# More held weights and an urgent last token block in a hybrid encoder layer: 40 slots instead of 24, the last block's norm ahead of other work, first products in k tiles

## The chip, the cores and the metric

The kernel runs on one core of a Trainium2 chip. The metric is device time in microseconds of one execution, as the median of several. The engines have one instruction queue each, which they work off in order: TensorE (PE; PEld is its weight load), VectorE (DVE), ScalarE (ACT), GpSimd (POOL) and SyncE (SP, here used to issue DMAs).

## The reference, cut to what matters

One encoder layer on 512 tokens of width 1024: two token mixers (windowed attention and a dilated mixture), merged by learned gates, then a layer norm, then a SwiGLU channel mixer with 2816 hidden columns, and a second layer norm.

```python
gates = jax.nn.sigmoid(h @ w_gate[l] + b_gate[l])
g_a, g_b = jnp.split(gates, N_BRANCH, axis=-1)
mixed = g_a * (o_a @ w_br_a[l]) + g_b * (o_b @ w_br_b[l])
y = mixed @ w_out[l]
h = layer_norm(DN_ALPHA * h + y, ln1_g[l], ln1_b[l])
f = (jax.nn.silu(h @ w_ff_gate[l]) * (h @ w_ff_up[l])) @ w_ff_down[l]
h = layer_norm(DN_ALPHA * h + f, ln2_g[l], ln2_b[l])
```

All of it is float32. The kernel writes each float32 operand as a high part and a low part and forms a product from three matmuls (high by high, high by low, low by high).

## The kernel before, in words

**A planner sets the order.** The kernel doesn't issue its instructions as it is written. It records operations (class Program, L95) with the engines they may run on, a cost for each engine, a priority (lower goes first), and what they read and write. The function run (L186) then plays a list schedule: at each moment it gives every free engine the ready operation of the lowest priority that fits the buffer limits, and emits it. So an engine's order comes out of the modelled costs, the priorities and the limits; on the chip each engine keeps that order and waits for whatever isn't there yet. There are limits on several classes of slots; "whl" is the number of slots that hold high and low parts of weights.

**The stretch that the change touches** begins after the mixers. First come the branch products with the gates (L930 to L944). Then comes w_out with the first layer norm (tok_major, L963): the tokens are four blocks t = 0 to 3 of 128, and each block has two column halves j = 0, 1 of 512. The last five of w_out's eight k tiles are taken block by block, so that a block's sum ends while the next ones are still computed. A block's norm is a chain on DVE with one step on ACT: residual (L998) and statistics (L1001) for either half, then the aggregate (L1004), the square root on ACT (L1006), the subtraction of the mean times the gain (L1012) for either half, the reciprocal (L1015), and the last step times reciprocal plus bias (L1023) for either half.

**turn_h1** (L1034) then turns each half into channel-major form: four 128 by 128 transposes on PE into one PSUM bank (L1042); the negated values as a high part (minus, L1050 on ACT or L1052 on DVE) and a low part (L1062, DVE); and two float32 copies by ACT into the tiles h1f (emitted at L322). The negated parts feed products on plain token halves; the h1f tiles are made into the sums and differences T1 to T4 (token_forms, L1095).

**The channel mixer** takes the hidden columns in 22 tiles of 128 (class Quad). A quad replaces the eight block products of a 2 by 2 splitting (columns and token halves) by seven, A11, A12, S1, S2, S3, S4 and A22, each 12 matmuls of 256 columns on weights or sums of weights; their token operands are B11, B21, T1, T2, T3, B22 and T4. A product is recorded in product (L1176), its matmuls stand at L1186 to L1188. Sums of weights, low parts of weights and the combinations of products all run at L1082 on DVE (tt); high parts run on ACT at L322. Some weight sums are accumulated by a DMA from POOL (L1140). The first three quads (N_HALF = 3) go in step: all their A11 and A12, then all S1, all S2 and so on. From quad 3 on they follow one by one, with pieces of the down projection (class Chunk) in between. T1 needs token block 3, while A11 and A12 need only blocks 0 and 1.

At the start of the branches free_all (L897) sets the limit of "whl" to 4 x 5 + 4 = 24. At the first silu of the channel mixer (L1211) it is set to 20. The PE order at the block that matters here was: A11 and A12 of quad 0, of quad 1, A11 of quad 2, the transposes of token block 3, A12 of quad 2, and then S1 of quad 0.

Of the kernel before, what the change touches and what calls it, by code (L numbers as in the profile page):

```python
# [16 lines left out]
S = 512  # L17
# [4 lines left out]
NR = 4  # L22
# [36 lines left out]
FIRST = {("k", 0): (-1000, -998.2, -997.2), ("q", 0): (-998.8, -998.1, -997.1), ("v", 0): (-998.7, -998, -997),  # L59
         ("k", 1): (-996.9,), ("q", 1): (-996.7,), ("v", 1): (-996.6,),  # L60
         "x": (-999.9, -998.5, -997.5, -996.95, -996.8, -996.5, -996.4, -996.3)}
N_WS, N_WHL, N_ATT = 6, 12, 16


N_CHUNK, N_PAIR, N_WF, N_WS2, N_WHL2 = 3, 3, 9, 9, 20
# [23 lines left out]


class Op:
    __slots__ = ("alts", "fn", "prio", "left", "ready", "succ", "bufs", "new", "done", "eng", "strict", "moves")


class Program:  # L95


    def __init__(self, limits):
        self.limits = limits
        self.used = {k: 0 for k in limits}  # L100
        self.ops = []
        self.writer, self.readers = {}, {}
        self.T = 0.0
        self.spare = SPARE
        self.strict = False

    @staticmethod
    def buf_of(tok):
# [1 line left out]

    def op(self, alts, fn, reads=(), writes=(), prio=0.0, after=(), abs_prio=None, moves=0.0):
        o = Op()
        o.alts, o.fn = alts, fn
        o.prio = (self.T + prio if abs_prio is None else abs_prio, len(self.ops))
        o.ready, o.done, o.eng = 0.0, None, None
        deps = set(a for a in after if a is not None)
        for t in reads:
            deps.update(self.writer.get(t, ()))
        for t in writes:
            deps.update(self.writer.get(t, ()))  # L120
            deps.update(self.readers.get(t, ()))
        deps.discard(o)
        for t in reads:
            self.readers.setdefault(t, []).append(o)
        for t in writes:
            self.writer[t] = [o]
            self.readers[t] = []
        o.bufs, o.new = [], []
        o.strict, o.moves = self.strict, moves
        for t in list(reads) + list(writes):  # L130
            b = self.buf_of(t)
            if b not in o.bufs:
                o.bufs.append(b)
# [32 lines left out]
    def run(self):  # L166
# [28 lines left out]
        while n_left:  # L195
            if not times:
                self.stuck(pending)
            now = heapq.heappop(times)
            while times and times[0] <= now:
                heapq.heappop(times)  # L200
            while frees and frees[0][0] <= now:
                _, _, b = heapq.heappop(frees)
                for key in b.keys:
                    if key in self.limits:
                        self.used[key] -= 1
            progress = True
            while progress:
                progress = False
                for e in engines:
                    if free[e] > now:  # L210
                        continue
                    best = None
                    for o in pending[e]:
                        if o.ready <= now and (best is None or o.prio < best.prio) and self.fits(o):
                            if e == DVE and len(o.alts) > 1 and free[ACT] < now + BIAS:
                                continue
                            best = o
                    if best is None:
                        continue
                    o = best  # L220
                    cost = dict(o.alts)[e]
                    for a, _ in o.alts:
                        pending[a].remove(o)
                    for b in o.bufs:
                        if b.tile is None:
                            b.tile = b.make()
                            for key in b.keys:
                                if key in self.limits:
                                    self.used[key] += 1
                    o.fn(e)  # L230
                    o.eng = e
                    if e == SP:
                        end = now + 0.06
                        dma[0] = max(dma[0], now) + 0.45
                        dma[1] = max(dma[1], dma[0] + 0.65) + cost
                        o.done = dma[1] + 0.9
                    elif o.moves:
                        end = now + cost
                        dma[1] = max(dma[1], end) + o.moves
                        o.done = dma[1] + 2.0  # L240
                    else:
                        end = now + cost
                        o.done = end
                    free[e] = end
                    heapq.heappush(times, end)
                    for b in o.bufs:
                        b.users -= 1
                        b.end = max(b.end, o.done)
                        if b.users == 0:
                            heapq.heappush(frees, (b.end + HOP, id(b), b))  # L250
                            heapq.heappush(times, b.end + HOP)
                    for q in o.succ:
                        same = len(q.alts) == 1 and q.alts[0][0] == e and e != SP and not o.moves
                        hop = SAME * (e in (ACT, DVE)) if same else HOP_PE if q.alts[0][0] == PE else HOP
# [26 lines left out]
def hybrid_layer(ctx: ExitStack, tc: tile.TileContext, wpack, xT, xtok, sink, bgate,  # L281
# [51 lines left out]
    def cp_alts(n, ps=False):  # L333
        return [(ACT, act(n, ps)), (DVE, dve(n, not ps))]
# [560 lines left out]
        step(w)  # L895

    def free_all(e):  # L897
        pr.limits.update(gen=N_SLOT - N_WS2 - N_WHL, ws=N_WS2, whl=max(N_WHL, 4 * N_LAST1 + 4))
        pr.spare = SPARE2

    op([(POOL, 0.0)], free_all, after=lasts)
# [61 lines left out]
    def tok_major(nk, last, us_of, u0, g, b, finish, fine, alpha=ALPHA):  # L963
# [22 lines left out]
                    kmm(k, t, j, 0, S, us, wu)  # L986
        res = [(k, us_of(k), unit(u0 + k)) for k in range(nk - last, nk)]
        for t in range(NR):
            st = stats()
            pieces = [(0, 0, S), (1, 0, S)]  # L990
            toks = []
# [28 lines left out]
            for (j, c0, c1), tok in zip(pieces, toks):  # L1020
                z = xt[t, j]
                op([(DVE, dve(c1 - c0, extra=0.06))], lambda e, z=z, st=st, j=j, c0=c0, c1=c1:
                   nc.vector.scalar_tensor_tensor(  # L1023
                       z.t[:, c0:c1], z.t[:, c0:c1], st.t[:, 35:36], b[j].t[:, c0:c1], op0=ALU.mult,
                       op1=ALU.add), reads=[tok, (st, "r"), b[j]], writes=[tok], prio=NOW)
                finish(t, j, c0, c1, tok)

    def copy_by_act(dst, src, n, ps, reads, writes, prio=EV):
        op([(ACT, act(n, ps))], lambda e: copy(ACT, dst(), src()), reads=reads, writes=writes, prio=prio)
# [5 lines left out]
    def turn_h1(t, j, c0, c1, tok):  # L1035
# [16 lines left out]
                nc.vector.tensor_scalar(h1h4[j].t[:, :, c], src(), -1.0, None, op0=ALU.mult)  # L1052

        alone = (j, t // 2) != (0, 1)
        if alone:
            op(cp_alts(S, True), minus, reads=[pb], writes=[(h1h4[j], t)], prio=NOW)
        for kk in range(2):
            x = h1f[j, t // 2][kk]
            copy_by_act(lambda x=x: x.t.rearrange("p (k c) -> p k c", k=2)[:, :, (t % 2) * P:(t % 2) * P + P],
                        lambda kk=kk: src()[:, 2 * kk:2 * kk + 2], 2 * P, True, [pb], [(x, t % 2)], NOW)  # L1060
        if alone:
            op([(DVE, dve(S, extra=0.1))], lambda e: nc.vector.scalar_tensor_tensor(  # L1062
                h1l4[j].t[:, :, c], src(), -1.0, f32(h1h4[j].t[:, :, c]), op0=ALU.mult, op1=ALU.subtract),
               reads=[pb, (h1h4[j], t)], writes=[(h1l4[j], t)], prio=NOW)

    lg, lb = ln_vectors(ln1g, ln1b, begin)
    tok_major(KD, N_LAST1, lambda k: sm[k], U_OUT, lg, lb, turn_h1, False)
# [31 lines left out]
    def token_forms():  # L1099
# [13 lines left out]
            tt(lambda: dst.t, lambda: x.t, lambda: y.t, ALU.subtract, al(x) + al(y), al(dst), S, prio)  # L1113

        p1, p2, p3, p4 = LOOK_T
        for x11, x12 in zip(b11, b12):
            diff(x11, x12, x11, p1)
        TP["T1"] = hl2(b11, p1)
        for x11, x12, x22 in zip(b11, b12, b22):
            diff(x12, x12, x22, p2)  # L1120
            diff(x22, x22, x11, p2)
# [22 lines left out]
    class Quad:  # L1144
# [33 lines left out]
        def product(self, s, b, ps, tok, c, first):  # L1178
            h, l = self.A[s]
            bh, bl, toks = tokens_of(b)  # L1180

            def go(e):
                o = ps.t[:, c]
                for k in range(4):
                    wh, wl = h.t[:, k * P:(k + 1) * P], l.t[:, k * P:(k + 1) * P]
                    mm(o, wh, bh[k](), start=(first and k == 0), stop=False, skip_group_check=True)  # L1186
                    mm(o, wh, bl[k](), start=False, stop=False, skip_group_check=True)  # L1187
                    mm(o, wl, bh[k](), start=False, stop=(k == 3), skip_group_check=True)  # L1188

            op([(PE, 12 * pe(HP))], go, reads=[h, l, *toks], writes=[(ps, tok)])  # L1190
            pr.T += 12 * pe(HP)

        def step(self, n):
            y, xz, t, v = self.y, self.xz, self.t, self.v
# [277 lines left out]
```

## Time and profile before

| | |
|---|---|
| median of 3 runs | 794.45 us (794.45 to 794.64) |
| the profiled execution | 793.29 us, span 791.5 us |
| granted TensorE clock | 0.997 |
| PE busy | 777.4 us, 98% |
| DVE busy | 665.9 us, 84% |
| ACT busy | 463.8 us, 59% |

A timeline row gives the start and the duration in us, the engine, the line and operation, output and inputs, partitions by elements, how many instructions the row holds, and in brackets the idle time ahead of it and what ended it. Matmuls overlap, so that the distance between two starts, not a duration, says what one of them costs PE. Groups of waits give the waiting line, the line waited for, the total in us, how many times, and the longest.

### The profile page before, as it was taken

To read this page: it belongs to the slowest core of one execution; us is meant where nothing else is said; L and a number is where in the kernel's file an instruction comes from. 1 tells how busy PE (TensorE), PEld (TensorE's weight loads), DVE (VectorE), ACT (ScalarE), POOL (GpSimd) and SP (SyncE) were. 2 spreads that over 40 slices of the span, in tenths; PEclk is the share of its full clock that TensorE was granted. 3 is DMA by queue.
4 is the path that set the end of the run, shared out by engine and by line. 5 is a ranking of instruction groups with operands and counts; after the bars stand their busy time and mean duration, and the time that the engine had idled before them with its cause. 6 is when DMAs were issued, how large, how long until landed. Compare 5 with 4: busy or idle time off the path is not lost.

```text
span 791.5 us, 13449 instructions
## 1 busy us (share of the span) xinstructions
PE 777.4 (98%) x4634; PEld 688.3 (87%) x4634; DVE 665.9 (84%) x1410; ACT 463.8 (59%) x1016; POOL 116.4 (15%) x284
## 2 busy tenths in 40 slices
PE   9999999999999999999999999999999999999995
PEld 6788888888998888888888889999999999999984
DVE  5998999899756999675585999988888889788888
ACT  5656675765855675795241487755655655555720
POOL 0000100000034000700011011034112330123000
PEclk9999999999999999999999999999999999999998
DMA  8524122421132122448343377779876977699202
GB/s 270 196 94 140 53 74 68 147 67 67 54 95 67 53 69 93 160 123 289 124 118 66 95 206 202 192 178 211 214 197 148 227 200 210 165 225 207 60 1 106
DMA packets 61125, 109.42 MB, mean 138 GB/s; under 512 B 7041, under 2 KB 8705, under 8 KB 61057
## 3 DMA queue, kind: packets, MB, share of 16 engines
q1 hardware_dynamic: 49392, 87.53, 33.8%
q0 software_dynamic: 11520, 20.98, 16.2%
q8 instruction: 36, 0.59, 0.3%
q14 instruction: 33, 0.26, 0.1%
q10 hardware_dynamic: 144, 0.07, 0.0%
HBM read 104.35 MB, written 4.19 MB: 137 GB/s over the span
## 4 chain that ended last, share of the span: by engine, by line
PE 84%; DVE 10%; DMA 2%; ACT 1%; issue 1%; SPq 1%; DVEq 0%; ACTq 0%
PE ps L443 11%; PE ps L445 11%; PE ps L444 11%; PE ps L1186 7%; PE ps L1188 7%; PE ps L1187 7%; DVE sl L1082 5%; PE ps L1313 4%; PE ps L1314 4%; PE ps L1315 4%; PE ps L621 3%; PE ps L528 2%; PE ps L527 2%; DMA sl<-wpack 2%; PE ps L976 1%; PE ps L974 1%
## 5 line engine op out<-in xcount | busy, mean ns | idle before, releaser
L322 ACT ACTIVATE sl<-sl 128x512 fp32r<-128x512 f32 (+3 forms) x421 | 234.2, 587 | 95.5 <-DVE sl L469 34.8
L1082 DVE TENSOR_TENSOR sl<-sl,sl 128x512 fp32r<-128x512 f32 (+3 forms) x308 | 171.6, 603 | 8.5 <-ACT sl L322 7.6
L322 ACT ACTIVATE sl<-ps 128x256 f32<-128x256 f32 (+5 forms) x189 | 83.3, 456 | 92.5 <-PE ps L1188 58.3
L443 PE MATMUL ps<-x,sl 128*128 128x512 f32 x336 | 133.6, 398 | 0.1
L444 PE MATMUL ps<-x,sl 128*128 128x512 f32 x336 | 131.6, 392 | 0.4 <-DVE x L419 0.2
L445 PE MATMUL ps<-x,sl 128*128 128x512 f32 x336 | 131.4, 391 | 0.0
L1186 PE MATMUL ps<-sl,sl 128*128 128x256 f32 x352 | 99.7, 283 | 0.9 <-ACT sl L322 0.9
L1187 PE MATMUL ps<-sl,sl 128*128 128x256 f32 x352 | 99.8, 284 | 0.8 <-DVE sl L1082 0.8
L1188 PE MATMUL ps<-sl,sl 128*128 128x256 f32 x352 | 99.6, 283 | 0.0
L343 DVE TENSOR_TENSOR sl<-sl,sl 128x512 fp32r<-128x512 f32 x130 | 87.1, 685 | 8.0 <-ACT sl L322 5.8
L1140 POOL DMA_DIRECT2D sl<-wpack x44 | 41.0, 1023 | 255.2 <-DVE sl L1082 107.4
L1186 PE MATMUL ps<-x,sl 128*128 128x256 f32 x264 | 75.0, 284 | 1.1 <-ACT sl L322 1.0
L445 PEld LDWEIGHTS ps<-x,sl 128*128 128x128 f32 x336 | 63.1, 188 | 13.8 <-DVE sl L371 0.2
L1187 PE MATMUL ps<-x,sl 128*128 128x256 f32 x264 | 74.7, 283 | 0.0
L1188 PE MATMUL ps<-x,sl 128*128 128x256 f32 x264 | 74.7, 283 | 0.0
L444 PEld LDWEIGHTS ps<-x,sl 128*128 128x128 f32 x336 | 63.3, 188 | 12.0 <-DVE x L419 1.3
L443 PEld LDWEIGHTS ps<-x,sl 128*128 128x128 f32 x336 | 63.2, 188 | 11.8 <-ACT x L322 1.0
L1186 PEld LDWEIGHTS ps<-sl,sl 128*128 128x128 f32 x352 | 67.5, 192 | 2.0 <-ACT sl L322 1.1
L1187 PEld LDWEIGHTS ps<-sl,sl 128*128 128x128 f32 x352 | 67.5, 192 | 1.8 <-DVE sl L1082 1.2
L1188 PEld LDWEIGHTS ps<-sl,sl 128*128 128x128 f32 x352 | 67.5, 192 | 0.0
L1082 DVE TENSOR_TENSOR sl<-sl,ps 128x512 f32<-128x512 f32 (+1 forms) x78 | 47.2, 610 | 23.1 <-PE ps L1188 14.4
L1186 PEld LDWEIGHTS ps<-x,sl 128*128 128x128 f32 x264 | 50.6, 192 | 2.0 <-ACT sl L322 1.5
(128 smaller groups left out, 1669.4 us busy)
## 6 DMA issues: line engine op xcount, KB each, us to landing
sl<-wpack SPq DMA_DIRECT2D x243, 256.0 KB, 4.0
sl<-wpack POOLq DMA_DIRECT2D x44, 256.0 KB, 5.5
wf<-wpack SPq DMA_DIRECT2D x36, 256.0 KB, 4.4
wf<-wpack POOLq DMA_DIRECT2D x36, 256.0 KB, 7.5
sl<-xT SPq DMA_DIRECT2D x8, 256.0 KB, 5.4
gz<-sl SPq DMA_DIRECT2D x8, 256.0 KB, 2.2
sl<-gz SPq DMA_DIRECT2D x8, 256.0 KB, 4.2
sl<-xtok SPq DMA_DIRECT2D x8, 256.0 KB, 5.4
```

What stands on the lines that cost most here:

```text
L322: nc.scalar.activation(dst, src, AF.Copy)
L343: op([(DVE, dve(S))], lambda e: nc.vector.tensor_tensor(l.t, src.t, f32(h.t), op=ALU.subtract), reads=[src, h], writes=[l], prio=prio, abs ...
L443: mm(o, a, x0, start=(k == 0), stop=False)
L444: mm(o, a, x1, start=False, stop=False)
L445: mm(o, b, x0, start=False, stop=(k == nk - 1))
L1082: op([(DVE, dve(w))], lambda e: nc.vector.tensor_tensor(dst(), x(), y(), op=o), reads=reads, writes=writes, prio=prio)
L1140: return op([(POOL, 1.0)], lambda e: nc.gpsimd.dma_start(dst.t, wpack[u, :, j * S:(j + 1) * S], accum_op=ALU.add), reads=[dst], writes=[ds ...
L1186: mm(o, wh, bh[k](), start=(first and k == 0), stop=False, skip_group_check=True)
L1187: mm(o, wh, bl[k](), start=False, stop=False, skip_group_check=True)
L1188: mm(o, wl, bh[k](), start=False, stop=(k == 3), skip_group_check=True)
L1313: mm(ps.t, x0, w[0].t, start=(first and m == 0), stop=False, skip_group_check=True)
L1314: mm(ps.t, x0, w[1].t, start=False, stop=False, skip_group_check=True)
```

## The change

There are four parts. The limit on held weight slots is 40 instead of 24 from the branches on. Operations of the last token block in tok_major, its transposes and h1f copies, and T1 carry a flag `urgent`: the planner doesn't start an operation without the flag on an engine if a flagged one of lower priority number becomes ready there before the first would end. In turn_h1 the two h1f copies are recorded ahead of the negation, and the negated parts of the last block get a later priority. The products A11 and A12 of the first three quads are recorded as four operations of three matmuls, one for each k tile, where they were one operation of twelve.

```diff
-N_WS, N_WHL, N_ATT = 6, 12, 16
+N_WS, N_WHL, N_ATT, N_WHL1 = 6, 12, 16, 40
...
         o = Op()
+        o.urgent = self.urgent
...
                     cost = dict(o.alts)[e]
+                    if not o.urgent and any(q.urgent and now < q.ready < now + cost and q.prio < o.prio
+                                            for q in pending[e]):
+                        continue
...
-        pr.limits.update(gen=N_SLOT - N_WS2 - N_WHL, ws=N_WS2, whl=max(N_WHL, 4 * N_LAST1 + 4))
+        pr.limits.update(gen=N_SLOT - N_WS2 - N_WHL, ws=N_WS2, whl=N_WHL1)
...
         for t in range(NR):
+            pr.urgent = t == NR - 1
             st = stats()
...
                 finish(t, j, c0, c1, tok)
+        pr.urgent = False
...
         alone = (j, t // 2) != (0, 1)
-        if alone:
-            op(cp_alts(S, True), minus, reads=[pb], writes=[(h1h4[j], t)], prio=NOW)
         for kk in range(2):
             x = h1f[j, t // 2][kk]
             copy_by_act(lambda x=x: x.t.rearrange("p (k c) -> p k c", k=2)[:, :, (t % 2) * P:(t % 2) * P + P],
                         lambda kk=kk: src()[:, 2 * kk:2 * kk + 2], 2 * P, True, [pb], [(x, t % 2)], NOW)
+        pr.urgent = False
         if alone:
+            later = LOOK_T[1] - 1 if t == NR - 1 else NOW
+            op(cp_alts(S, True), minus, reads=[pb], writes=[(h1h4[j], t)], prio=later)
             op([(DVE, dve(S, extra=0.1))], lambda e: nc.vector.scalar_tensor_tensor(
                 h1l4[j].t[:, :, c], src(), -1.0, f32(h1h4[j].t[:, :, c]), op0=ALU.mult, op1=ALU.subtract),
-               reads=[pb, (h1h4[j], t)], writes=[(h1l4[j], t)], prio=NOW)
+               reads=[pb, (h1h4[j], t)], writes=[(h1l4[j], t)], prio=later)
+        pr.urgent = t == NR - 1
...
         p1, p2, p3, p4 = LOOK_T
+        pr.urgent = True
         for x11, x12 in zip(b11, b12):
             diff(x11, x12, x11, p1)
         TP["T1"] = hl2(b11, p1)
+        pr.urgent = False
...
-            def go(e):
+            def go(e, ks=range(4)):
...
-            op([(PE, 12 * pe(HP))], go, reads=[h, l, *toks], writes=[(ps, tok)])
-            pr.T += 12 * pe(HP)
+            n = 1 if s in ("A11", "A12") and self.f < N_HALF else 4
+            for k in range(0, 4, n):
+                op([(PE, 3 * n * pe(HP))], lambda e, k=k: go(e, range(k, k + n)), reads=[h, l, *toks], writes=[(ps, tok)])
+                pr.T += 3 * n * pe(HP)
```

What this does to the order shows at three places. The lines of the changed kernel lie 5 to 13 higher: L998 is L1004, L1001 is L1007, L1012 is L1018, L1023 is L1029, L1042 is L1049, L1062 is L1070, L1082 is L1091, L1186 is L1197, L1211 is L1224, L322 is L327.

DVE, from the second half's statistics of token block 3 to the end of its norm, before. L1082 rows are low parts of weights, st is the block's statistics, and the two sl tiles at L1012 and L1023 are the block's halves:

```order
L1001 BN_STATS st_5114<-sl_4448 128x6
L1082 TENSOR_TENSOR sl_5084<-sl_4825,sl_5083 128x512
L1004 BN_AGGR st_5114<-st_5114 128x2
L1082 TENSOR_TENSOR sl_5092<-sl_4851,sl_5091 128x512
L1012 SCALAR_TENSOR_TENSOR sl_4446<-sl_4446,st_5114,sl_4450 128x512
L1012 SCALAR_TENSOR_TENSOR sl_4448<-sl_4448,st_5114,sl_4452 128x512
L1015 RECIPROCAL st_5114<-st_5114 128x1
L1082 TENSOR_TENSOR sl_5099<-sl_4856,sl_5098 128x512
L1023 SCALAR_TENSOR_TENSOR sl_4446<-sl_4446,st_5114,sl_4454 128x512
L1023 SCALAR_TENSOR_TENSOR sl_4448<-sl_4448,st_5114,sl_4456 128x512
```

And now, with the low part of block 2 (L1070) within the chain, and behind it the one weight split and the two differences of T1:

```order
L1007 BN_STATS st_5168<-sl_4655 128x6
L1010 BN_AGGR st_5168<-st_5168 128x2
L1018 SCALAR_TENSOR_TENSOR sl_4652<-sl_4652,st_5168,sl_4662 128x512
L1070 SCALAR_TENSOR_TENSOR x_5031<-ps_5177,x_5024 128x4x128
L1018 SCALAR_TENSOR_TENSOR sl_4655<-sl_4655,st_5168,sl_4665 128x512
L1021 RECIPROCAL st_5168<-st_5168 128x1
L1029 SCALAR_TENSOR_TENSOR sl_4652<-sl_4652,st_5168,sl_4672 128x512
L1029 SCALAR_TENSOR_TENSOR sl_4655<-sl_4655,st_5168,sl_4674 128x512
L1091 TENSOR_TENSOR sl_5115<-sl_4893,sl_5114 128x512
L1091 TENSOR_TENSOR sl_5006<-sl_5173,sl_5006 128x512
L1091 TENSOR_TENSOR sl_5013<-sl_5175,sl_5013 128x512
```

The weight splits have left the chain; they now stand ahead of token block 0's norm.

PE at the transposes of token block 3, before. The rows ahead of them end A11 of quad 2, those behind begin A12 of quad 2:

```order
L1187 MATMUL ps_5205<-x_4968,sl_5068 128x256
L1188 MATMUL ps_5205<-x_4959,sl_5069 128x256
L1042 MATMUL ps_5221<-ident,sl_4446 128x128 x4
L1042 MATMUL ps_5229<-ident,sl_4448 128x128 x4
L1186 MATMUL ps_5237<-x_4975,sl_5077 128x256
```

And now; the rows ahead end A11 of quad 1, those behind begin A12 of quad 1:

```order
L1198 MATMUL ps_5228<-x_5026,sl_4783 128x256
L1199 MATMUL ps_5228<-x_5008,sl_4784 128x256
L1049 MATMUL ps_5246<-ident,sl_4652 128x128 x4
L1049 MATMUL ps_5253<-ident,sl_4655 128x128 x4
L1197 MATMUL ps_5259<-x_5024,sl_4791 128x256
```

The transposes stand behind 36 product matmuls instead of 60; 36 instead of 12 follow them up to S1 of quad 0.

ACT around the copy of quad 3's product S1 out of PSUM, before. It is the second row from the end; the silu is that of quad 2, and the rows between are high parts for the down projection, which need the quads' results:

```order
L322 ACTIVATE sl_5666<-ps_5637 128x256
L1211 ACTIVATE sl_5226<-sl_5226 128x512
L322 ACTIVATE sl_5672<-sl_5200 128x256
L322 ACTIVATE sl_5687<-sl_5163 128x256
L322 ACTIVATE sl_5691<-sl_5200 128x256
L322 ACTIVATE sl_5694<-sl_5226 128x256
L322 ACTIVATE sl_5710<-ps_5653 128x256
L322 ACTIVATE sl_5713<-sl_5696 128x256
```

And now, with the same copy in the last row:

```order
L1224 ACTIVATE sl_5312<-sl_5312 128x512
L327 ACTIVATE sl_5662<-sl_5244 128x256
L327 ACTIVATE sl_5679<-sl_5420 128x512
L327 ACTIVATE sl_5685<-ps_5624 128x256
L327 ACTIVATE sl_5689<-sl_5222 128x256
L327 ACTIVATE sl_5692<-sl_5244 128x256
L327 ACTIVATE sl_5706<-sl_5483 128x512
L327 ACTIVATE sl_5713<-sl_5312 128x256
L327 ACTIVATE sl_5729<-sl_5460 128x512
L327 ACTIVATE sl_5735<-ps_5664 128x256
```

The silu has moved ahead of the copy of quad 3's first product, and three high parts of weights (128x512 rows without a PSUM input) now stand between it and the copy of S1. From some quads further on the order of all engines is the same in both kernels up to the end.

More of the change, by code (lines that the diff above doesn't have):

```diff
@@ L91 @@
 class Op:
-    __slots__ = ("alts", "fn", "prio", "left", "ready", "succ", "bufs", "new", "done", "eng", "strict", "moves")
+    __slots__ = ("alts", "fn", "prio", "left", "ready", "succ", "bufs", "new", "done", "eng", "strict", "moves", "urgent")
 class Program:
@@ L105, in __init__ @@
         self.strict = False
+        self.urgent = False
     @staticmethod
@@ L1180, in product @@
             bh, bl, toks = tokens_of(b)
-            def go(e):
+            def go(e, ks=range(4)):
                 o = ps.t[:, c]
-                for k in range(4):
+                for k in ks:
                     wh, wl = h.t[:, k * P:(k + 1) * P], l.t[:, k * P:(k + 1) * P]
```

## The prediction

> **What bounds the kernel now.** I read the page's busy times first, then TensorE's waits, then busy time by stretches of 20 us, and last single rows of the timelines where PE stood still.
>
> ```profile
> PE 777.4 (98%) x4634; PEld 688.3 (87%) x4634; DVE 665.9 (84%) x1410; ACT 463.8 (59%) x1016; POOL 116.4 (15%) x284
> ...
> PE ps L1186 <- ACT sl L322: 1.9, 2, 1.0
> ...
> PE ps L1187 <- DVE sl L1082: 0.8, 2, 0.5
> PE ps L1042 <- DVE sl L1023: 0.4, 2, 0.2
> ...
> 360.00:380.00 20.00, 20.00 (x90) 16.57 (x89) 9.58 (x16) 7.03 (x13) 0.00 (x0) 1.00 0.73 261
> ...
> 440.00:460.00 20.00, 18.29 (x123) 16.34 (x122) 19.50 (x35) 12.57 (x31) 1.75 (x2) 1.00 0.49 134
> ...
> 480.00:500.00 20.00, 18.87 (x154) 18.33 (x153) 20.00 (x46) 14.09 (x34) 3.51 (x4) 1.00 0.68 161
> 500.00:520.00 20.00, 20.00 (x169) 20.00 (x168) 17.94 (x35) 14.10 (x31) 4.96 (x6) 1.00 0.56 143
> ```
>
> TensorE is the bound: the same 4634 matmuls run in both kernels at a granted clock of 1.00, so this change can only win back time in which PE stands still. (In a stretch's row the columns after its length are the busy us of PE, PEld, DVE, ACT and POOL, then clock, DMA share and GB/s.) PE lacks 1.71 us in 440 to 460 and 1.13 in 480 to 500, and in both DVE is full (19.50 and 20.00), while at 360 to 380 DVE was busy only 9.58 of 20. At 500 to 520 PE is full again. The places, row by row:
>
> ```profile
> 435.84 0.39 PE L975 MATMUL ps<-sl,sl 128*128 128x512 f32 x1
> 436.07 0.39 PE L976 MATMUL ps<-sl,sl 128*128 128x512 f32 x1
> 436.66 1.38 PE L1042 MATMUL ps<-ident,sl 128*128 128x128 f32 x8 [0.21 <-DVE sl L1023]
> ...
> 445.86 0.39 PE L976 MATMUL ps<-sl,sl 128*128 128x512 f32 x1
> 446.48 0.63 PE L1042 MATMUL ps<-ident,sl 128*128 128x128 f32 x4 [0.23 <-DVE sl L1023]
> ...
> 447.41 0.39 PE L976 MATMUL ps<-sl,sl 128*128 128x512 f32 x1
> ...
> 447.99 0.36 PE L1186 MATMUL ps<-x,sl 128*128 128x256 f32 x1
> ...
> 455.26 1.03 PE L1042 MATMUL ps<-ident,sl 128*128 128x128 f32 x8
> 456.05 0.36 PE L1186 MATMUL ps<-x,sl 128*128 128x256 f32 x1
> ...
> 457.33 0.28 PE L1187 MATMUL ps<-x,sl 128*128 128x256 f32 x1
> 457.45 0.28 PE L1188 MATMUL ps<-x,sl 128*128 128x256 f32 x1
> 458.68 0.38 PE L1186 MATMUL ps<-sl,sl 128*128 128x256 f32 x1 [0.95 <-ACT sl L322]
> 459.59 0.38 PE L1187 MATMUL ps<-sl,sl 128*128 128x256 f32 x1 [0.53 <-DVE sl L1082]
> ...
> 461.49 0.28 PE L1186 MATMUL ps<-sl,sl 128*128 128x256 f32 x1
> ```
>
> Matmuls follow each other every 0.12 us at 256 columns (457.33, 457.45) and every 0.23 at 512 (435.84, 436.07), so starts tell what a stop cost. The transposes of token block 1 were due at 436.30 and began at 436.66: 0.36 lost. Those of block 2 were due at 446.09, began at 446.48: 0.39 lost. The large one: the first product on T1 (S1 of quad 0) was due at 457.57, and the next product begins at 461.49. Its 12 matmuls need 1.44, so 461.49 - 457.57 - 1.44 = **2.48 lost**, on T1's high part from ACT and its low part from DVE. T1 is late because the last block's norm was late:
>
> ```profile
> 432.65 0.68 DVE L998 SCALAR_TENSOR_TENSOR sl<-sl,ps 128x512 f32<-128x512 f32 x1
> ...
> 435.86 1.41 DVE L1023 SCALAR_TENSOR_TENSOR sl<-sl,st,sl 128x512 f32<-128x512 f32 x2
> ...
> 448.10 0.69 DVE L998 SCALAR_TENSOR_TENSOR sl<-sl,ps 128x512 f32<-128x512 f32 x1
> 448.70 0.69 DVE L1082 TENSOR_TENSOR sl<-sl,sl 128x512 fp32r<-128x512 f32 x1
> 449.45 0.69 DVE L1062 SCALAR_TENSOR_TENSOR x<-ps,x 128x512 fp32r<-128x512 f32 x1
> ...
> 453.33 0.67 DVE L1082 TENSOR_TENSOR sl<-sl,sl 128x512 fp32r<-128x512 f32 x1
> 453.92 1.41 DVE L1023 SCALAR_TENSOR_TENSOR sl<-sl,st,sl 128x512 f32<-128x512 f32 x2
> ```
>
> From the second residual (L998) to the last L1023's end, block 1 takes 435.86 + 1.41 - 432.65 = 4.62 us with nothing between. The last block takes 453.92 + 1.41 - 448.10 = 7.23, with weight splits (L1082, about 0.60 each from start to start: 453.33 to 453.92) among its steps.
>
> **The change, part by part.**
>
> *Limit 40 instead of 24.* About ten weight splits of quads 0 to 2 now stand ahead of block 0's norm on DVE; 10 x 0.60 = 6 us, into a region with 10.4 idle us in one stretch of 20. Cost on PE: nothing, since PE is at 20.00 there with DVE half empty; if that cover were gone, at most those 6 us would move to block 0's norm. SP issues some FF weights ahead of the token loads:
>
> ```profile
> sl<-xtok SPq DMA_DIRECT2D x8, 256.0 KB, 5.4
> ...
> 420.63 0.69 DVE L998 SCALAR_TENSOR_TENSOR sl<-sl,ps 128x512 f32<-128x512 f32 x1 [7.10 <-PE ps L976]
> ```
>
> At 261 GB/s a 256 KB load takes 1.0 us, so even twenty put ahead delay the tokens by 20 us from the 360s, to before 390; they are first used at 420.63. Cost zero.
>
> *Copies before the negation.* In blocks 0 and 1 one negation moves from ACT to DVE, between two ACT copies of the same bank. ACT and DVE take turns there already:
>
> ```profile
> 430.86 0.38 ACT L322 ACTIVATE sl<-ps 128x256 f32<-128x256 f32 x1 [0.76 <-DVE x L1062]
> ```
>
> So the move gains only the order of turns: stepping through block 0's bank with these durations, block 1's second residual comes 0.24 earlier. Bounds: 0.76 earlier (one turn saved) or 0.1 later (DVE's 0.68 for ACT's 0.60). I take 0.24, nearest to what the listing allows. It shortens the 0.36 before block 1's transposes by **0.24**; block 2 inherits it and gains another 0.24, 0.48 in all, against 0.39 lost: **0.39** back. Hence the first product begins at 447.99 - 0.63 = 447.36.
>
> *Last block ahead.* PE's last w_out matmul ends at 447.41 + 0.39 - 0.63 = 447.17, so the residual starts at about 447.25. One other instruction (the low part, 0.60) is left within the chain: 447.25 + 4.62 + 0.60 = 452.47 for the last norm row instead of 455.33, **2.86 earlier**. Bounds: 4.62 with nothing between, 7.23 as before. PE now has these transposes after 36 product matmuls instead of 60, at 447.36 + 36 x 0.12 = 451.68. The first half of the block is finished about 0.7 before the second, at 451.8, so the two groups of four wait about 0.2 each, as at 436.66 and 446.48: **-0.40**, a new stall (between 0 and, with the old chain, 455.33 - 452.47 = 2.86 more).
>
> T1: after the last norm row DVE has one split (0.60), two differences (1.20), then the low parts behind ACT's high parts: 452.47 + 0.6 + 1.2 + 0.6 + 0.6 and two hand-overs of 0.1 = 455.7. PE reaches S1 of quad 0 at 457.57 - 0.63 + 0.40 = 457.34, 1.6 us later than that. The **2.48** go to zero. The next product starts at 458.78 instead of 461.49.
>
> *k tile by k tile.* Same matmuls, same instructions: cost zero, by the 0.12 between starts within and across products. It only lets the planner slip the transposes in; in the listing they still lie between whole products.
>
> *Quad 3.* Here an earlier queue decides.
>
> ```profile
> 487.29 0.28 PE L1188 MATMUL ps<-sl,sl 128*128 128x256 f32 x1
> 488.56 0.38 PE L1186 MATMUL ps<-x,sl 128*128 128x256 f32 x1 [1.00 <-ACT sl L322]
> ...
> 498.81 0.28 PE L1188 MATMUL ps<-sl,sl 128*128 128x256 f32 x1
> 499.22 0.38 PE L1186 MATMUL ps<-x,sl 128*128 128x256 f32 x1
> ...
> 477.07 1.28 ACT L1211 ACT_TABLE_LOAD   x1 [1.99 <-DVE sl L1082]
> 478.37 0.63 ACT L1211 ACTIVATE sl<-sl 128x512 f32<-128x512 f32 x1
> ...
> 485.82 0.63 ACT L1211 ACTIVATE sl<-sl 128x512 f32<-128x512 f32 x1 [2.15 <-DVE sl L1082]
> ...
> 488.15 0.36 ACT L322 ACTIVATE sl<-ps 128x256 f32<-128x256 f32 x1
> ```
>
> S4 of quad 3 was due at 487.41, began at 488.56: 1.15 lost on the copy at 488.15, which stood in ACT's queue behind a silu that waited 2.15 for a full DVE. With some 6 us of splits done earlier, that silu's input no longer comes last: I place the copy's end at 484.1 to 484.4, and S4 is due at 487.41 - 2.71 = 484.70. So **1.15** comes back, with 0.3 to 0.6 spare. Bounds: 0 to 1.15. At S4 of quad 4 another 0.29 is lost (due 498.93, begun 499.22); its row names no releaser, so I count nothing back there, with bounds of 0 and 0.29.
>
> That spare holds the table load ahead of the first silu: 1.28 us, and silu starts 0.02 behind it. (The Trainium skill, page "ScalarE activation: ScalarE: Activation LUTs", section "What ACT_TABLE_LOAD costs", puts a switch at about 2.66 us, a drain of 1.38 included. By it the copy would come some 1.4 later and the 1.15 would stay, so the sum would be the first rival's. The 0.02 speaks against the drain behind the load; ACT had idled 1.99 before it, where a drain ahead could hide.)
>
> **Sum**: 0.24 + 0.39 - 0.40 + 2.48 + 1.15 = 3.86 off the profiled execution (793.29, a span of 791.5 and 1.8 around it), which gives 789.4; it lies 1.16 below the median of 794.45, so a median of 794.45 - 3.86 = **790.6**.
>
> **Rivals.** *Quad 3 stays late*: 794.45 - 2.71 = 791.7. For it: DVE's 20.00 there, ACT's strict order, a spare of 0.3 to 0.6. Against: the work taken out ahead of it. *The wait only moves*: if the last block's chain keeps its 7.23, PE stands in front of the transposes placed earlier for 2.61 us (7.23 against 5.22) more; 2.71 - 2.61 leaves 0.1, so 794.35 with quad 3 late. For it: PE runs in order, and 24 matmuls that covered the norm now stand behind it. Against: four of five foreign instructions are gone from the chain. *Slower*: at the first silu the weights' limit falls to 20, as before, now from 40; if the splits of later quads then start late, each quad stops as S4 did, 1.15 apiece. From quad 3 to quad 8 that is 6 x 1.15 = 6.9, of which 1.15 is there already; less the gain of 2.71 it makes 3.04 more: 797.5. It decides once three quads more than now stop (3 x 1.15 = 3.45 exceeds 2.71). For: DVE is full at 480 to 500. Against: from 500 on PE is at 20.00 with DVE at 17.94, and the listing has the order of the later quads unchanged. That the change does nothing is ruled out by the listing.
>
> **How the numbers follow.** Forecast 0.50, quad 3 late 0.27, wait moved 0.16, slower 0.07. The range goes from 789.6 to 793.0. Below the forecast lie the new stall (0.40), the 0.12 left at block 1, quad 4's 0.29 and the 0.19 by which the runs shown differ; above it lie the first rival and half of the way from there to the second. A measurement tells about 0.2%, 1.6 us: faster 0.79 (forecast, first rival, a little of the second), same 0.14, slower 0.07.
>
> **What would show it.** Right: no PE wait on L1186's T1 parts; one other instruction between the last block's second residual and its last norm row, some 5.2 us apart; PE waiting about 0.2 twice before that block's transposes; no stop before S4 of quad 3. Wrong: a wait of over 1 us at those transposes (second rival), a stop at S4 of quad 3 (first), or PE below 20.00 in stretches after 500 (slower).

## The result

The changed kernel takes **789.12 us** (median of 6, 788.04 to 789.70) against 794.43 (median of 6, 793.45 to 794.64): a ratio of 0.9933, with a 95% interval of 0.9921 to 0.9946. That is faster by 5.3 us, of which the interval leaves 4.3 to 6.3. The forecast was 790.6, with a range from 789.6 to 793.0: the direction was right, and the gain was larger than the range allowed.

TensorE's waits in the profile of the changed kernel (waiting line, line waited for, total, times, longest):

```profile
PE ps L403 <- DVE eps L435: 1.2, 1, 1.2
PE ps L448 <- ACT x L327: 0.8, 2, 0.7
PE ps L565 <- ACT sl L327: 0.8, 1, 0.8
PE ps L449 <- DVE x L424: 0.2, 1, 0.2
```

Every one of these stands ahead of the stretch that the change touches. The waits at the products on ACT and DVE and those at the transposes are gone from the list. Busy time by stretches, in the same columns as before:

```profile
420.00:440.00 20.00, 19.89 (x96) 16.22 (x95) 15.38 (x27) 3.49 (x11) 0.00 (x0) 1.00 0.10 32
440.00:460.00 20.00, 19.99 (x137) 18.13 (x137) 19.10 (x34) 15.11 (x35) 1.72 (x2) 1.00 0.43 108
460.00:480.00 20.00, 20.00 (x169) 20.00 (x168) 19.99 (x36) 11.59 (x24) 3.48 (x4) 1.00 0.91 265
480.00:500.00 20.00, 20.00 (x169) 20.00 (x168) 19.65 (x44) 15.44 (x36) 3.48 (x4) 1.00 0.68 184
```

PE is at 19.99 and 20.00 in the stretches where it had 18.29 and 18.87. DVE is as full as it was, 19.10 and 19.65: it does nearly the same work (three instructions more, which ACT has fewer), in another order. The rows at the places that the prediction named, on PE, DVE and ACT in turn:

```profile
437.06 0.39 PE L981 MATMUL ps<-sl,sl 128*128 128x512 f32 x1
437.46 1.38 PE L1049 MATMUL ps<-ident,sl 128*128 128x128 f32 x8
...
452.63 0.28 PE L1199 MATMUL ps<-x,sl 128*128 128x256 f32 x1
452.84 1.32 PE L1049 MATMUL ps<-ident,sl 128*128 128x128 f32 x8
453.91 0.36 PE L1197 MATMUL ps<-x,sl 128*128 128x256 f32 x1
...
458.19 0.28 PE L1199 MATMUL ps<-x,sl 128*128 128x256 f32 x1
458.31 0.28 PE L1197 MATMUL ps<-sl,sl 128*128 128x256 f32 x1
...
485.55 0.28 PE L1199 MATMUL ps<-sl,sl 128*128 128x256 f32 x1
485.67 0.28 PE L1197 MATMUL ps<-x,sl 128*128 128x256 f32 x1
...
495.63 0.28 PE L1199 MATMUL ps<-sl,sl 128*128 128x256 f32 x1
495.75 0.28 PE L1197 MATMUL ps<-x,sl 128*128 128x256 f32 x1
```

```profile
448.21 0.69 DVE L1004 SCALAR_TENSOR_TENSOR sl<-sl,ps 128x512 f32<-128x512 f32 x1 [0.27 <-PE ps L981]
...
452.03 1.42 DVE L1029 SCALAR_TENSOR_TENSOR sl<-sl,st,sl 128x512 f32<-128x512 f32 x2
```

```profile
471.75 3.75 ACT L327 ACTIVATE sl<-sl 128x512 fp32r<-128x512 f32 x7
475.51 1.28 ACT L1224 ACT_TABLE_LOAD   x1
476.81 0.64 ACT L1224 ACTIVATE sl<-sl 128x512 f32<-128x512 f32 x1
...
484.43 0.38 ACT L327 ACTIVATE sl<-ps 128x256 f32<-128x256 f32 x1
```

S1 of quad 0 begins at 458.31, S4 of quad 3 at 485.67 and S4 of quad 4 at 495.75, each 0.12 after the matmul ahead of it: no stop. Only the transposes still cost something, 0.17 at block 1 (437.06 + 0.23 = 437.29 was due, 437.46 came) and, at the last block, 0.09 in front and 1.07 instead of 0.79 for the eight. The last norm takes 452.03 + 1.42 - 448.21 = 5.24 us where it took 7.23.

**The gain by place.** Both kernels run 4634 matmuls, so the n-th start of one can be set against the n-th start of the other. That takes the first 424 us out, in which the change doesn't alter PE's work. Counted from the 2191st matmul (423.83 before, 424.83 after), the change has won 0.63 at the transposes of blocks 1 and 2, has lost 0.36 at those of block 3, has won 2.47 in the products of quads 0 to 2 and 1.83 from quad 3 on. The 2801st matmul stands at 511.79 before and at 508.23 after: 87.96 us less 83.39 before rounding, which is **4.57 us**, and it stays 4.57 to the end. All gains by place below are counted in this way against the kernel before; they come from one profile of each kernel. Two profiles of the changed kernel give 4.57 and 4.57. Such a count compares like with like only where both kernels have the same kinds of matmuls behind them. So the places end where every kernel here has done the same ones: at the 2330th matmul (behind the transposes of block 2), at the 2384th (the last before S1 of quad 0), at the 2600th (in quad 3) and at the 2801st.

### The profile page after: what moved, and what is told of

The parts are those of the page before. It is cut to its first block, busy times and chain, and to the rows that moved or that the text cites. A ratio compares the mean times of both kernels' runs of the same rounds, so it can differ in the third digit from the quotient of the medians.

```text
span 787.9 us, 13456 instructions
## 1 busy us (share of the span) xinstructions
PE 776.5 (99%) x4634; PEld 688.3 (87%) x4634; DVE 668.6 (85%) x1413; ACT 463.6 (59%) x1013; POOL 116.9 (15%) x284
## 4 chain that ended last, share of the span: by engine, by line
PE 92%; DVE 3%; DMA 3%; ACT 1%; SPq 0%; issue 0%; DVEq 0%
PE ps L448 11%; PE ps L449 11%; PE ps L450 11%; PE ps L1199 9%; PE ps L1198 9%; PE ps L1197 9%; PE ps L1326 4%; PE ps L1327 4%; PE ps L1328 4%; PE ps L626 3%; PE ps L979 2%; PE ps L981 2%; PE ps L980 2%; PE ps L533 2%; PE ps L532 2%; DMA sl<-xT 1%
## 5 line engine op out<-in xcount | busy, mean ns | idle before, releaser
L327 ACT ACTIVATE sl<-sl 128x512 fp32r<-128x512 f32 (+3 forms) x420 | 234.0, 587 | 88.4 <-DVE sl L474 34.6
L1091 DVE TENSOR_TENSOR sl<-sl,sl 128x512 fp32r<-128x512 f32 (+3 forms) x308 | 171.9, 603 | 8.7 <-ACT sl L327 7.7
L327 ACT ACTIVATE sl<-ps 128x256 f32<-128x256 f32 (+5 forms) x189 | 83.4, 457 | 103.2 <-PE ps L1199 65.0
L1199 PE MATMUL ps<-sl,sl 128*128 128x256 f32 x352 | 99.6, 283 | 0.0
L1197 PE MATMUL ps<-sl,sl 128*128 128x256 f32 x352 | 99.5, 283 | 0.0
L1197 PE MATMUL ps<-x,sl 128*128 128x256 f32 x264 | 74.8, 283 | 0.0
L1199 PE MATMUL ps<-x,sl 128*128 128x256 f32 x264 | 74.7, 283 | 0.0
L1091 DVE TENSOR_TENSOR sl<-sl,ps 128x512 f32<-128x512 f32 (+1 forms) x78 | 47.2, 610 | 25.0 <-PE ps L1199 15.7
L1197 PEld LDWEIGHTS ps<-sl,sl 128*128 128x128 f32 x352 | 67.5, 192 | 0.8
L1199 PEld LDWEIGHTS ps<-sl,sl 128*128 128x128 f32 x352 | 67.5, 192 | 0.0
L1197 PEld LDWEIGHTS ps<-x,sl 128*128 128x128 f32 x264 | 50.6, 192 | 0.5
```

The lines of the kernel that those rows point to most:

```text
L327: nc.scalar.activation(dst, src, AF.Copy)
L1091: op([(DVE, dve(w))], lambda e: nc.vector.tensor_tensor(dst(), x(), y(), op=o), reads=reads, writes=writes, prio=prio)
```

## The experiments

| kernel | blocks 1, 2 | block 3's transposes | quads 0 to 2 | from quad 3 on | sum |
|---|---|---|---|---|---|
| the change | 0.63 | -0.36 | 2.47 | 1.83 | 4.57 |
| limit 40 alone | 0.01 | 0.00 | 0.01 | 0.82 | 0.83 |
| limit 40, turn_h1 | 0.63 | 0.00 | 1.18 | 1.83 | 3.63 |
| limit 40, turn_h1, k tiles | 0.63 | 0.00 | 1.81 | 0.71 | 3.15 |
| all but turn_h1 | 0.01 | -0.52 | 2.47 | 1.83 | 3.79 |
| all but the limit (24) | 0.59 | -1.68 | -1.24 | 1.29 | -1.05 |
| limit 32 | 0.63 | -0.55 | 2.47 | 1.25 | 3.79 |
| limit 48 | 0.63 | -0.57 | 2.47 | 1.29 | 3.83 |
| flag on all blocks | 0.60 | -0.46 | 2.47 | 1.45 | 4.06 |
| negation on ACT | 1.11 | 0.01 | 2.47 | 1.67 | 5.26 |
| both of these | 1.11 | -0.44 | 2.47 | 1.83 | 4.97 |

The change without the k tiles isn't in the table and was not run: its listing has the same operations in the same order on every engine as the change, so beside the flag the k tiles change nothing.

**The limit alone.**

```diff
-        pr.limits.update(gen=N_SLOT - N_WS2 - N_WHL, ws=N_WS2, whl=max(N_WHL, 4 * N_LAST1 + 4))
+        pr.limits.update(gen=N_SLOT - N_WS2 - N_WHL, ws=N_WS2, whl=40)
```

> The kernel before with the limit of held weight slots at 40 and nothing else of the change. Its listing keeps four weight splits inside the last block's norm and three between that norm and T1's differences, as before. Theory (the limit pays at quads 3 and 4, through a shorter DVE backlog; the flag pays at T1): the stop before S1 of quad 0 stays at about 2.4 us, the stops at S4 of quads 3 and 4 (1.15 and 0.29, with refill 1.83 in all) go: 794.4 - 1.8 = 792.6. Rival (the limit alone brings T1 forward too, since DVE has 6 us less to do): 789.8. Second rival (the limit does nothing by itself): 794.4.

Measured: 792.54 us against 793.82 (ratio 0.9985, 0.9976 to 0.9994). The time is that of the theory by luck: the kernel before ran at 793.82 here, 0.6 below the 794.4 that the theory started from. The gain is 1.28 by the medians and 0.83 by place, not 1.8, since the stop at S4 of quad 3 didn't go. PE, and ACT ahead of it, in this kernel:

```profile
487.16 0.28 PE L1188 MATMUL ps<-sl,sl 128*128 128x256 f32 x1
488.20 0.38 PE L1186 MATMUL ps<-x,sl 128*128 128x256 f32 x1 [0.76 <-ACT sl L322]
```

```profile
485.15 0.36 ACT L322 ACTIVATE sl<-ps 128x256 f32<-128x256 f32 x1
485.44 0.42 ACT L322 ACTIVATE sl<-sl 128x256 fp32r<-128x256 f32 x1
486.45 0.42 ACT L322 ACTIVATE sl<-sl 128x256 fp32r<-128x256 f32 x1 [0.59 <-DVE sl L1289]
487.12 0.75 ACT L322 ACTIVATE sl<-sl 128x256 fp32r<-128x256 f32 x2 [0.25 <-DVE sl L1289]
487.78 0.64 ACT L322 ACTIVATE sl<-ps 128x256 f32<-128x256 f32 x2
```

0.92 of the 1.15 remains (due at 487.28, begun at 488.20). ACT made the copy of quad 3's first product at 485.15. It then stood before high parts for the down projection, which wait for DVE's sums (L1289), and came to the copy of S1 only at 487.78. So six us of splits out of the way is not enough; what stands in ACT's queue ahead of that copy counts too. The 0.82 that this kernel wins from quad 3 on are 0.24 there and the two small stops behind it, at S3 of quad 3 (0.19) and S4 of quad 4 (0.39).

**Everything but the limit.**

```diff
-N_WS, N_WHL, N_ATT, N_WHL1 = 6, 12, 16, 40
+N_WS, N_WHL, N_ATT, N_WHL1 = 6, 12, 16, 24
```

> The changed kernel with the limit back at 24. The listing has no weight split inside the last block's norm, but the ten splits stand behind T1 instead of ahead of block 0's norm. Theory: T1's stop is gone (2.4 less the 0.3 lost at the transposes), blocks 1 and 2 keep their 0.6, and the stops at S4 of quads 3 and 4 stay: 794.4 - 2.7 = 791.7. Rival (the limit isn't needed, the flag does all): 789.1. Second rival (the splits pushed behind T1 stop PE at A12 and S1 of quads 0 to 2): 793 or more.

Measured: 795.35 against 793.82 (ratio 1.0018, 1.0009 to 1.0027): slower than the kernel before. The theory's 791.7 falls, and the second rival holds. The rows in which PE waits from block 3's transposes to quad 2:

```profile
458.57 0.39 PE L1199 MATMUL ps<-x,sl 128*128 128x256 f32 x1 [0.81 <-DVE sl L1091]
...
466.45 0.39 PE L1197 MATMUL ps<-sl,sl 128*128 128x256 f32 x1 [0.30 <-ACT sl L327]
...
467.60 0.39 PE L1199 MATMUL ps<-sl,sl 128*128 128x256 f32 x1 [0.64 <-DVE sl L1091]
...
472.99 0.39 PE L1197 MATMUL ps<-sl,sl 128*128 128x256 f32 x1 [1.05 <-ACT sl L327]
473.80 0.39 PE L1199 MATMUL ps<-sl,sl 128*128 128x256 f32 x1 [0.31 <-DVE sl L1091]
```

The first of these (L1199 needs the low part of a weight) is a product on plain tokens: the weight split that the flag had pushed behind T1 is now itself late. The others lie in later products of quads 0 to 2. The flag doesn't remove work from DVE, it only exchanges it. With 24 slots the pushed work cannot have been done earlier, and its price is more than T1's stop was. In the table, 1.07 of the 1.68 lost at block 3 is the stop at that first product. S4 of quad 3 has no stop here, with a limit of 24: PE reached it 2.3 us later, counted from the 2191st matmul, than it was due before, while the copy that it needs ended only 0.4 later. So the 1.29 from quad 3 on come from the earlier losses.

**No flag.**

```diff
-        o.urgent = self.urgent
+        o.urgent = False
```

> The changed kernel without the flag (no operation is held back for an urgent one); limit 40, the copies ahead of the negation and the k tiles stay. The listing has four weight splits inside the last block's norm again. Theory: the stop before S1 of quad 0 returns with about 2.1 us and quads 3 and 4 stay free: 789.1 + 2.1 = 791.2, up to 792.0. Rival (the flag is idle once the limit is 40): 789.1.

Measured: 790.36 against 793.82 (ratio 0.9955, 0.9942 to 0.9969). Neither story fits. By place the products of quads 0 to 2 lose 0.67 against the change, not 2.1, and S4 of quad 3 loses 1.11, where the theory had nothing. By the medians the gain of 3.46 is near the theory's 3.2, by luck. So the flag is worth 4.57 - 3.15 = 1.4 us, and most of T1's stop goes without it.

**Without the new order in turn_h1.**

```diff
         alone = (j, t // 2) != (0, 1)
+        later = NOW
+        if alone:
+            op(cp_alts(S, True), minus, reads=[pb], writes=[(h1h4[j], t)], prio=later)
         for kk in range(2):
...
-            later = LOOK_T[1] - 1 if t == NR - 1 else NOW
-            op(cp_alts(S, True), minus, reads=[pb], writes=[(h1h4[j], t)], prio=later)
```

> The changed kernel with turn_h1 as it was before (the negation recorded ahead of the h1f copies, the last block's negated parts at the usual priority); limit, flag and k tiles stay. Theory: the 0.6 us won at the transposes of blocks 1 and 2 is lost, T1 comes some 0.6 later on ACT but within its slack of 1.6: 789.1 + 0.6 = 789.7. Rival (the order in turn_h1 changes nothing): 789.1. Second rival (T1 has no such slack): 790.4.

Measured: 789.58 against 793.82 (ratio 0.9946, 0.9933 to 0.9958). The theory holds: 0.62 lost at blocks 1 and 2, 0.16 at block 3's transposes, nothing behind them, since T1 has slack.

**The limit and turn_h1, without flag and k tiles.**

```diff
-        o.urgent = self.urgent
+        o.urgent = False
...
-            n = 1 if s in ("A11", "A12") and self.f < N_HALF else 4
+            n = 4
```

> The kernel before with the limit at 40 and the new order in turn_h1, without the flag and without the k tiles. The listing has the last block's transposes behind 60 product matmuls again, against 54 without the flag alone. Theory (without the flag the k tiles do work, since they let the transposes go 6 x 0.12 = 0.72 us earlier): from the branches to the end 2.4 us less than before, against 3.15 without the flag alone, with a stop of 1.2 to 1.3 at S1 of quad 0. Rival (the k tiles do nothing): 3.15 again, with 0.57 at that stop.

Measured by place: 3.63, not 2.4. The expected part is there: without the k tiles quads 0 to 2 win 0.63 less than with them (1.18 against 1.81), with a stop of 1.29 at S1 of quad 0. But the whole of quad 3's and 4's 1.83 is there too, where the kernel with k tiles has 0.71. Without the flag the k tiles win at T1 and lose more at quad 3, so there they are worth -0.48. And turn_h1's order, which has 0.63 by itself at blocks 1 and 2, is worth 2.80 beside the limit (0.83 to 3.63), but 0.78 beside limit and flag.

**The spare time of the copy before S4 of quad 3.** In the changed kernel ACT makes that copy three or seven times.

```diff
-                copy_by_act(lambda: v.t[:, HI], lambda: xz.t[:, HI], HP, True, [(xz, "z")], [(v, 2)])
+                op([(ACT, act(HP, True))], lambda e: [copy(ACT, v.t[:, HI], xz.t[:, HI])
+                                                      for _ in range(3 if self.f == 3 else 1)],
+                   reads=[(xz, "z")], writes=[(v, 2)], prio=EV)
```

> The changed kernel in which ACT makes the copy of quad 3's product S1 out of PSUM three times instead of once, all else in the same order: the copy ends 2 x 0.27 = 0.54 us later. In the changed kernel's profile it ended at 484.81 and PE began S4 of quad 3 at 485.67 without a stop; a hand-over took 0.05 before (488.51 to 488.56), so 0.8 is spare. Theory (spare of 0.8): no stop at S4 of quad 3, at most 0.1. Rival (the forecast's spare of 0.3 to 0.6): a stop of 0 to 0.25.

> The same with seven copies instead of one: 6 x 0.27 = 1.62 us later. Theory (spare of 0.8): a stop of 0.8 at S4 of quad 3, and 0.8 to 1.0 us on the whole. Rival (forecast's spare): 1.0 to 1.3. Second rival (ACT's later copies come late too and each quad's stop adds up): over 1.5.

A repeated copy took 0.42 us and not 0.27, because each writes the same tile and waits for the one before: the seven copies

```profile
483.89 2.88 ACT L327 ACTIVATE sl<-ps 128x256 f32<-128x256 f32 x7
```

end at 486.77 where a single one (0.38) would have ended at 484.27, a delay of 2.50. PE, in this kernel:

```profile
485.01 0.28 PE L1199 MATMUL ps<-sl,sl 128*128 128x256 f32 x1
486.82 0.39 PE L1197 MATMUL ps<-x,sl 128*128 128x256 f32 x1 [1.54 <-ACT sl L327]
```

stops for 486.82 - 485.13 = 1.69. ACT and PE in the kernel with three copies:

```profile
483.44 1.22 ACT L327 ACTIVATE sl<-ps 128x256 f32<-128x256 f32 x3
```

```profile
484.56 0.28 PE L1199 MATMUL ps<-sl,sl 128*128 128x256 f32 x1
484.71 0.39 PE L1197 MATMUL ps<-x,sl 128*128 128x256 f32 x1
```

Here the delay is 1.22 - 0.38 = 0.84 and the stop 484.71 - 484.68 = 0.03. So 2.50 - 1.69 = 0.81 and 0.84 - 0.03 = 0.81: the spare is 0.81, and past it this copy delays PE one for one. The sums are 4.45 and 2.79, so a stop there isn't made up later.

**Other limits.** The same line as above with 32 and with 48.

> The changed kernel with a limit of 32 slots. The listing has seven to nine of the ten splits ahead of block 0's norm, and the last block's transposes behind 42 product matmuls. Theory (the flag pays only so far as the splits that it pushes aside are already done): between the gains of limits 24 (-1.05 us from the branches to the end) and 40 (4.57), nearer to 40: 3 to 4 us. Rival (any limit over 24 will do): 4.5.

> The changed kernel with a limit of 48 slots. The listing has four more weight splits ahead of block 0's norm and one inside block 0's; the last block's transposes stand behind 42 product matmuls. Theory (at 40 DVE's backlog no longer stops PE, so more slots bring nothing): 4.4 to 4.6 us. Rival (the split inside block 0's norm delays blocks 1 and 2): 4.0.

Measured by place: 3.79 and 3.83. 32 slots carry most of the gain, as the theory had it; 48 lose, against the theory, but not at the norm (0.63 as ever): both have block 3's transposes six matmuls later and lose 0.2 there, and 0.58 and 0.53 from quad 3 on. More slots than the work needs aren't neutral, because they change the order.

**The flag on all blocks, the negation on ACT, and both.**

```diff
-            pr.urgent = t == NR - 1
+            pr.urgent = True
...
-            op(cp_alts(S, True), minus, reads=[pb], writes=[(h1h4[j], t)], prio=later)
+            op([a for a in cp_alts(S, True) if a[0] == ACT], minus, reads=[pb], writes=[(h1h4[j], t)], prio=later)
```

> The changed kernel with the flag on all four token blocks instead of the last. The listing has no weight split inside block 2's norm either, and the last block's transposes behind 39 product matmuls. In the changed kernel about 0.9 us is still lost between the branches and quad 0's S1: 0.17 and 0.26 at block 1, 0.28 at the last block, the rest refill. Theory (what's left is the norm's own length in blocks 0 and 1, not foreign work): 4.5 to 4.7 us from the branches to the end, as with the change (4.57). Rival (foreign work is what delays the last block): 4.9.

> The changed kernel with the negation always on ACT, so that ACT and DVE no longer change places twice on one bank in blocks 0 and 1. DVE loses 0.6 us of work in each of the two blocks. Theory: the stop before block 1's transposes (0.17) goes and the last block is finished up to 0.3 earlier: 4.7 to 4.9 us. Rival (the order of turns on the bank, not the work, sets the time, as the forecast had it): 4.3, since DVE's low part must now wait for a third ACT operation.

> Both of these edits together: flag on all four blocks, negation always on ACT. Theory: 4.7 to 5.0 us from the branches to the end. Rival: no more than the better of the two.

Measured by place: 4.06, 5.26 and 4.97. The flag on all blocks misses theory and rival alike: it wins nothing at blocks 1 and 2 (0.60 against 0.63, with the same stops of 0.17 and 0.26 at block 1), and loses 0.10 at block 3's transposes and 0.38 at S4 of quad 3. The negation on ACT beats its theory: it wins 0.47 at blocks 1 and 2 and 0.37 at block 3, loses 0.16 at S4 of quad 3, and no stop over 0.12 is left from the w_out products to the end of the SwiGLU's first quads. With the flag on all blocks beside it, block 3 loses 0.45 of that again, so both together are no better than the negation alone.

**The change and that version, timed together.**

> The changed kernel once more. Theory (the change is worth what PE's starts show from the branches to the end, 4.57, and the rest of the 5.31 between the first medians is scatter of the first 360 us): 4.2 to 4.9 us below the kernel before. Rival (the change also shortens the part ahead of the branches): 5.1 to 5.6 below.

> The changed kernel with the negation always on ACT, timed. Theory (its profile's 5.26 against 4.57 from the branches to the end holds): 0.7 us below the change, 5.0 to 5.5 below the kernel before. Rival (one profile isn't enough, the two are alike): within 0.2 of the change.

Measured, against 793.59 for the kernel before on that chip: the change 788.74 (ratio 0.9936, 0.9922 to 0.9949), 4.85 less; the negation on ACT 787.60 (ratio 0.9925, 0.9912 to 0.9937), 5.99 less. The change is where the theory put it. The other version gained more than its theory's 5.0 to 5.5 and lies 1.14 under the change by medians of five and 0.70 by place in its second profile (5.27 against 4.57). The two ranges of single runs overlap (787.11 to 788.63 and 787.90 to 789.32), and the two intervals as well, so its lead rests on the places in two profiles of each more than on the times. Of all that ran it is the fastest.

## Why the prediction was right or wrong

The direction, the mechanism at T1 and the two largest terms were right. The size was too small, and a part of the reasoning was right for a wrong reason.

| term | predicted | measured |
|---|---|---|
| block 1's transposes | 0.24 | 0.21 |
| block 2's transposes | 0.39 | 0.42 |
| last block's transposes | -0.40 | -0.36 |
| S1 of quad 0 | 2.48 | 2.47 |
| S4 of quad 3 | 1.15 | 1.25 |
| S3 of quad 3 | not in the sum | 0.19 |
| S4 of quad 4 | 0 | 0.39 |
| sum | 3.86 | 4.57 |

*The steps that failed.* First, "At S4 of quad 4 another 0.29 is lost ...; its row names no releaser, so I count nothing back there". It came back, with 0.39. The missing name was no reason to think that the stop had another cause than the one a quad before. Second, S4 of quad 3 was sized by the late start alone: 1.15. The start behind a stop is late as well (488.56 to 488.79 before, where 0.12 is usual), and with this refill of 0.10 the place gave 1.25. The same refill was left out at quad 4. Third, the next product of quad 3, S3, had a small stop of its own that the prediction doesn't mention. The rows before, on PE and on ACT:

```profile
489.97 0.28 PE L1188 MATMUL ps<-x,sl 128*128 128x256 f32 x1
490.18 0.39 PE L1186 MATMUL ps<-sl,sl 128*128 128x256 f32 x1
490.40 0.28 PE L1187 MATMUL ps<-sl,sl 128*128 128x256 f32 x1
```

```profile
489.76 0.36 ACT L322 ACTIVATE sl<-ps 128x256 f32<-128x256 f32 x1
...
498.80 0.36 ACT L322 ACTIVATE sl<-ps 128x256 f32<-128x256 f32 x1
```

S3 was due at 490.09 and began at 490.18, 0.06 after the copy of S2 out of the same bank had ended (489.76 + 0.36 = 490.12); with the refill it lost 0.19. The second ACT row is the copy of quad 4's S1. It ended at 499.16, 0.06 before S4 of quad 4 began at 499.22, so that the stop without a name has the same cause. Together these make 0.39 + 0.10 + 0.19 = 0.68 of the 0.71 that the sum lacks.

*The rest is the base.* The measured 5.31 is 1.45 more than the sum: 0.71 are the terms, and 0.74 is a difference that the places don't show. The forecast took its terms off a median of three runs, 794.45, which lay 0.6 above the median of 21 later ones (793.82). When change and kernel before were timed together again, the change was 4.85 faster. The first comparison so holds some 0.5 to 0.7 us that did not come again; the range had allowed 0.19 for this, the spread of the three runs it knew. With all terms right the forecast would have been 794.45 - 4.57 = 789.9, within the range: what carried the result out of it is terms and base together. Whether these 0.5 to 0.7 us are chance or a difference between chips is not shown.

*What had the wrong reason.* "With some 6 us of splits done earlier, that silu's input no longer comes last": the limit alone does these splits earlier and keeps 0.92 of the stop. What decides is whether the copy ends before PE gets there, and that followed from the whole order: the copy ended 1.10 us after S4 was due in the kernel before, 0.87 after it with the limit alone and 0.95 after it without the flag, but 0.86 ahead of it in the changed kernel and 0.28 ahead with the limit and turn_h1, though in that last kernel ACT also waits for DVE three times (0.25, 0.25 and 0.41) between the silu of quad 2 and the copy. No run singles out which operation ahead of the copy sets its time. The placing itself was good: the copy's end was forecast for 484.1 to 484.4 on the time scale of before, and came at 484.81 - 1.01 = 483.80, with 0.81 to spare for the 0.3 to 0.6 of the forecast. And the move of two negations from ACT to DVE, counted as part of a gain of 0.24 a block, costs: with them on ACT the two blocks win 1.11 instead of 0.63. The gain there was that of the copies' place alone.

*The table load.* It took 1.28 us from 475.51, right behind high parts on ACT that ended at 471.75 + 3.75 = 475.50, and silu began at 476.81. So it cost 1.31 on a busy engine. The Trainium skill, page "ScalarE: Activation LUTs", section "What ACT_TABLE_LOAD costs", counts about 1.38 more for a drain. No such time shows here on either side of the load: the measurement decides, and the load did not make the copy late.

*The rivals.* "Quad 3 stays late" did not come about, but it does with small edits: without the flag 1.1 us of it is back. "The wait only moves" came true for 0.36 at block 3, which the sum had with 0.40. As a rival it was priced wrongly: 7.23 - 5.22 is 2.01, not 2.61, so it stood at 793.75 and not at 794.35. "Slower" came about in the experiment with the limit at 24, by another road than the one forecast: the splits of quads 0 to 2 were the late ones, not those of later quads.

## What to carry to other kernels

Urgency for one chain only exchanges work on a full engine: look for what is pushed aside and whether it can be done earlier; here all parts but the slots lost 1.05 us and with them gained 4.57, though the slots alone were worth 0.83. Size a stop by the distance between two work items that both kernels share, refill included, and for a stop that names no releaser look up what ended just ahead of it. When a queue's order comes from a planner, a small edit can move a late item elsewhere, so measure parts together as well as alone.

## What the runs showed of the hardware that I had not expected

PE works off the same first 1900 matmuls in all kernels here, yet the 1901st began between 357.56 and 359.30 us in 16 profiles (358.09 before, 359.10 and 358.12 in the two of the change). All of this spread is there at the 118th matmul, which began between 31.27 and 32.97; from there to the 1901st each profile took 326.2 to 326.3 us. So 1.7 us of difference between two single profiles' spans can come from the first 33 us, from work that neither changed. The distance from a common matmul on agrees within 0.02 us between two profiles of the same kernel.
